# RWKV inverses in a two-layer mixer kernel: forward substitution in blocks of 8 instead of 16, and one more doubling level on TensorE

## The chip, the cores and the metric

The kernel runs on one core of a Trainium2 chip. The metric is device time in microseconds (us) of one execution, lower is better. The kernel before takes 2290.6 us, the median of three runs (2287.16 to 2292.19).

## The reference: two mixer layers, of which RWKV-7 is one of four branches

A layer normalises 256 text tokens and 1024 image tokens of 1024 channels, projects them, sends the result through four mixers (RWKV-7, S5, SSD, GLA), and projects the mixers' outputs back with a norm, a gate and a residual sum. The change lies in RWKV-7. Its reference is a scan over tokens, for two directions and four heads of 64 channels:

```
def step(S, inp):
    r_t, w_t, k_t, v_t, kk_t, a_t = inp
    sa = jnp.einsum('bhvk,bhk->bhv', S, -kk_t)
    S = S * w_t[:, :, None, :] + sa[..., None] * (kk_t * a_t)[:, :, None, :] + v_t[..., None] * k_t[:, :, None, :]
    y = jnp.einsum('bhvk,bhk->bhv', S, r_t) if need_out else None
    return S, y
...
y = ys[0] + ys[1]
mu = jnp.mean(y, axis=-1, keepdims=True)
var = jnp.mean(jnp.square(y - mu), axis=-1, keepdims=True)
y = ((y - mu) * lax.rsqrt(var + RW_GN_EPS)).reshape(b, L, W_BR) * p['rw_ln_w'] + p['rw_ln_b']
y = y + (bonus[0] + bonus[1]).reshape(b, L, W_BR)
return y * jax.nn.silu(gate), (finals[0], finals[1])
```

The kernel does not scan token by token. It takes 64 tokens at once: with A the strictly triangular 64 x 64 matrix of interactions between the tokens of such a chunk, all updates of the chunk follow from one multiplication by T = inverse(I - A).

## The kernel before: ten windows in a pipeline of five stages, laid out by a scheduler

After the in-projection and the other mixers of a layer, `rw` runs ten windows. A window is 128 tokens forward and 128 tokens backward, that is two chunks (`s`) of two directions with four heads, 16 inverses of 64 x 64 in all. Five functions make a window's stages: `rw_elem` (decays, scaled keys; DVE, ACT, POOL), `rw_pair` (the interactions A, on TensorE into the PSUM tag `pb`, masked by DVE), `rw_inv` and `rw_vals` (the inverses, the values by token), `rw_chain` (the recurrence over chunks, which multiplies by the inverse `r_TT` on PE into `pu`), `rw_out` and `rw_final`. In one iteration of the loop each stage works on another window (`ORDER`), and jobs of the S5 mixer (tiles `z_...`) go along in seven of the iterations (`SJ`).

The program text is only the input: a scheduler orders each engine's instructions by priorities and by durations that it assumes, and fixes that order when the kernel is built. So an edit of `rw_inv` can move everything that stands in the same phase.

`rw_inv` before the change: the 32 x 32 diagonal blocks of A lie in `r_Ad`, four to a column of 128 partitions. A DVE transpose writes them out with the matrix along the free axis (`r_N`), and forward substitution runs on the 16 x 16 diagonal blocks, held in `r_X`. For i = 15 down to 1 it issues two DVE instructions, a product into `r_tp` and a sum into `r_X`, each dependent on the one before:

```
for i in range(15, 0, -1):
    r0 = i // 4
    ...
    self.tt(tmp[:, :, :i, r0:], N[:, :, i, 0:i]..., X[:, :, i:i + 1, r0:4]..., OP.mult)
    self.tt(X[:, :, :i, r0:4], X[:, :, :i, r0:4], tmp[:, :, :i, r0:], OP.add)
```

Two DVE transposes make `r_DT` and `r_DN` of the result. Then two doublings follow, each of two rounds of small matmuls through the one bank of the PSUM tag `pi`. The first goes from blocks of 16 to blocks of 32: `r_Am` (the off-diagonal part of `r_Ad`, picked by POOL with a mask) times `r_DN`, an ACT copy to `r_Rm`, `r_Rm` times `r_DT`, a DVE sum into `r_DT`, a DVE transpose to `r_DN`. The second goes from 32 to 64 (`r_Bb`, `r_Rb`) into `r_TT`. A round of the first is 32 calls of 32 x 32 x 32. All of them are in f32 and show as two instructions each. Buffers: `r_Ad`, `r_N`, `r_X`, `r_Am`, `r_Rm` one each, `r_DT` and `r_DN` two, `r_A` three, PSUM tag `pi` one bank.

Of the kernel before, what the change touches and what calls it, by code (L numbers as in the profile page):

```python
# [32 lines left out]
# ---------------------------------------------------------------- column layout of w_in  # L33
# [30 lines left out]
# ---------------------------------------------------------------- per-layer parameter columns  # L64
# [21 lines left out]
# ---------------------------------------------------------------- constants that depend on shapes alone  # L86
# all along, for the projections and mixers, for RWKV
CON, ACON, RCON = {}, {}, {}
for _d, _l in ((CON, [("ident", 128), ("ones", 128), ("bones", 128), ("eps", 1), ("gneps", 1), ("one", 1)]),
               (ACON, [("triF", 128), ("triB", 128), ("gmF", 64), ("gmB", 64), ("bm4", 4), ("c16", 16), ("reset64", 256)]),  # L90
               (RCON, [("IJ", 128), ("vinit", 256), ("rm", 128), ("m16", 32), ("reset64", 256)])):
# [10 lines left out]
def constants():  # L102
# [27 lines left out]
    put("IJ", ij)  # L130
    put("m16", (np.arange(128) % 32 < 16)[:, None] & (np.arange(32) >= 16)[None])
# [92 lines left out]
# PSUM banks by tag: projections of the first layer and of the others, RWKV, out-projection  # L224
# [4 lines left out]
# tiles of a channel tile's size, of 512 columns, of S5's tables  # L229
NT_, NQ_, NH_ = (8,11,6)  # L230
# stages of the RWKV pipeline, as traced; iterations that S5 goes along with
ORDER = (3, 2, 4, 1, 0)
SJ = (3,5,6,7,9,10,11)
# order of the mixers by layer: p, q tables of S5 for this layer and the next, g GLA, s SSD, r inputs of RWKV
MO = ('pqgsr', 'gsr')
# SBUF pools from the left | from the right, by layer: what ends early lies where the next phase begins
RL = ('sm rp rl hp tp qp|re rx', 're hp tp qp rx|rp sm rl')
CL = ('oy oo ob|oa', 'oa oy oo|ob')
# engines of the residual sums and of the squares of the normed output, by pair of channel tiles
RA = "pvpv"  # L240
AA = "ppvv"
# engines of RWKV's elementwise work, by step: a ACT, p GpSimd, v DVE
EG = dict(bk="aa", ad="pppp", dg="aaaa", bb="pp", b0="p", b1="v", tk="pp", am="p", ar="vp", sp="p", bt="aa")
# tiles of the RWKV phase by size, buffers of its output
RN = (3, 2, 10)
NF = 2
# buffers of the weights, tiles projected first, by layer
WB = (4, 6)
G1 = ("misc gk", "misc gk gq")
# engines of the decays within a chunk of SSD, by direction and part  # L250
LE = "vvvv"
# order of the pools of the first layer
# [3 lines left out]
class K:  # L256
# [17 lines left out]
    def load_con(self, rwkv):  # L274
        """the constants and matrices of a phase"""
# [8 lines left out]
    def pools(self, es, nts=0, nq=0, nh=0, left=(), right=(), **psum):  # L284
        """the pools of a phase: by name, from either end of SBUF; PSUM banks by tag"""
# [23 lines left out]
    def ring(self, name, shape, n):  # L309
        """n tiles in turn, zeroed once: what is written later leaves the zeros alone"""  # L310
        ts = [self.Q(name, shape) for _ in range(n)]
        for t in ts:
            self.nc.gpsimd.memset(t, 0.0)
        return itertools.cycle(ts)
# [1499 lines left out]
```

## Time and profile before

| what | before |
|---|---|
| runs, median (lowest to highest) | 2290.6 us (2287.16 to 2292.19) |
| profiled execution, span | 2282.5 us |
| median of the runs less this span | 8.1 us |
| PE busy | 1955.0 us (86%) |
| PE weight loads busy | 1642.1 us (72%) |
| DVE busy | 1565.4 us (69%) |
| ACT busy | 933.8 us (41%) |
| POOL busy | 830.7 us (36%) |
| RWKV phase of the first layer, about | 735 to 1142 us |
| RWKV phase of the second layer, about | 1772 to 2181 us |

The profiled execution has no time of its own in the record besides its span. The span runs from its first to its last instruction; what lies around the span is in the runs' times. The two RWKV phases have 816 us between them. The engines' names: PE is TensorE, DVE VectorE, ACT ScalarE, POOL GpSimd, SP the engine that issues most DMAs.

### The profile page before, as it was taken

How to read it: one execution, taken by the hardware profiler on the slowest of the kernel's cores; microseconds unless marked ns; L12 is line 12 of the kernel's file. 1: busy time of each engine (PE TensorE's matmuls, PEld its weight loads, DVE VectorE, ACT ScalarE, POOL GpSimd, SP SyncE). 2: the span in 40 equal slices, each digit the busy share in tenths (PEclk: the TensorE clock that was granted, in tenths of full speed). 3: DMA queues.
4: the chain of work that ended last, by engine and by line, in shares of the span. 5: the costliest groups of instructions: out<-in, count | busy, mean ns of one | idle time of the engine just before them, and what ended most of it. 6: DMA issues, size and time to landing. Idle time of an engine off the chain costs nothing.

```text
span 2282.5 us, 44172 instructions
## 1 busy us (share of the span) xinstructions
PE 1955.0 (86%) x17176; PEld 1642.1 (72%) x17176; DVE 1565.4 (69%) x3513; ACT 933.8 (41%) x2016; POOL 830.7 (36%) x947
## 2 busy tenths in 40 slices
PE   7788898999975587878899999999996567888997
PEld 5577787778743466766799888887884456767797
DVE  3986867547495888897647724366665799987654
ACT  3445222223442554645423326122463456565420
POOL 1434753302246444553332203220136355454322
PEclk8689999999997688979999999999997678899898
DMA  8133544224454322422233423132412432220432
GB/s 281 44 116 122 179 152 136 65 91 140 149 164 136 112 83 80 121 64 68 94 116 94 137 90 133 55 99 86 146 50 73 145 97 85 80 75 25 139 112 93
DMA packets 208481, 246.79 MB, mean 108 GB/s; under 512 B 28816, under 2 KB 150672, under 8 KB 208272
## 3 DMA queue, kind: packets, MB, share of 16 engines
q1 hardware_dynamic: 175264, 215.52, 29.8%
q10 hardware_dynamic: 33008, 28.45, 3.8%
q8 instruction: 135, 2.21, 0.4%
q14 instruction: 74, 0.61, 0.1%
HBM read 169.29 MB, written 76.71 MB: 108 GB/s over the span
## 4 chain that ended last, share of the span: by engine, by line
PE 36%; DVE 17%; ACT 6%; issue 3%; DMA 3%; POOL 2%; SPq 0%; ACTq 0%; DVEq 0%; POOLq 0%
PE pj L321 22%; PE ps L321 3%; PE px L321 2%; PE pu L321 2%; DVE r_tp L333 2%; DVE r_X L333 2%; PE pb L321 2%; PE pc L321 1%; PE pi L321 1%; DVE r_N L1276 1%; DVE r_cs L1195 1%; PE p L321 1%; DVE z_x L333 1%; DVE r_BK L333 1%; ACT r_th L330 1%
## 5 line engine op out<-in xcount | busy, mean ns | idle before, releaser
L321 PE MATMUL pj<-hi,i_wh 128*128 128x512 f32 (+1 forms) x952 | 243.8, 377 | 18.6 <-DVE hi L1516 12.0
L321 PE MATMUL pj<-lo,i_wh 128*128 128x512 f32 (+1 forms) x952 | 240.2, 370 | 1.3 <-POOL lo L333 1.3
L321 PE MATMUL pj<-hi,i_wl 128*128 128x512 f32 (+1 forms) x952 | 239.1, 369 | 0.1
L321 PEld LDWEIGHTS pj<-hi,i_wh 128*128 128x128 f32 x952 | 169.1, 196 | 52.3 <-DVE hi L1516 12.4
L321 PEld LDWEIGHTS pj<-lo,i_wh 128*128 128x128 f32 x952 | 167.3, 193 | 32.5 <-issue 1.5
L321 PEld LDWEIGHTS pj<-hi,i_wl 128*128 128x128 f32 x952 | 167.0, 192 | 31.2 <-issue 2.6
L333 DVE TENSOR_TENSOR i_wl<-i_w,i_wh 128x512 fp32r<-128x512 f32 x108 | 82.6, 772 | 107.8 <-PE pj L321 59.9
L1539 ACT CAST i_wh<-i_w 128x512 fp32r<-128x512 f32 x108 | 66.4, 620 | 159.0 <-PE pj L321 113.4
L321 PE MATMUL pb<-r_AD,r_BK 128*128 128x256 f32 x320 | 99.9, 464 | 19.9 <-DVE r_tp L333 9.4
L321 PE MATMUL px<-r_UV,r_A 128*64 128x64 f32 x1216 | 103.9, 240 | 14.1 <-DVE r_UV L1376 10.5
L321 PEld LDWEIGHTS px<-r_UV,r_A 128*64 128x64 f32 x1216 | 88.1, 150 | 35.0 <-DVE r_UV L1376 14.6
L321 PEld LDWEIGHTS pb<-r_AD,r_BK 128*128 128x128 f32 x320 | 72.0, 237 | 37.6 <-issue 11.9
L333 DVE TENSOR_TENSOR r_X<-r_X,r_tp 128x30 f32<-128x30 f32 (+1 forms) x300 | 89.8, 299 | 6.7
L333 DVE TENSOR_TENSOR r_tp<-r_N,r_X 128x30 f32<-128x30 f32 (+1 forms) x300 | 87.6, 292 | 6.6
L321 PE MATMUL pu<-r_rs,r_TT 128*64 128x128 f32 x320 | 51.2, 311 | 35.0 <-ACT r_rs L1372 35.0
L330 ACT ACT_TABLE_LOAD x56 | 71.8, 1283 | 11.6 <-DMA z<-in_s5p 4.6
L330 ACT ACTIVATE i_o<-pj,omu 128x512 f32<-128x512 f32 (+1 forms) x46 | 28.5, 622 | 115.4 <-PE pj L321 113.8
L333 DVE TENSOR_TENSOR g_Y<-pc,g_Y 64x256 f32<-64x256 f32 x70 | 29.5, 421 | 65.0 <-ACT g_Y L536 35.3
L333 POOL TENSOR_TENSOR r_S<-r_S,r_PM 64x256 f32<-64x256 f32 x72 | 53.0, 737 | 56.6 <-DVE r_S L333 43.1
L321 PE MATMUL pj<-i_wh,hi 128*128 128x256 f32 x448 | 67.2, 288 | 6.4 <-ACT i_o L330 4.0
L336 POOL TENSOR_SCALAR r_AD<-r_AR 64x512 f32<-64x512 f32 (+1 forms) x80 | 56.7, 709 | 40.8 <-PE pb L321 31.9
L321 PEld LDWEIGHTS pu<-r_rs,r_TT 128*64 128x64 f32 x320 | 40.1, 155 | 41.4 <-ACT r_rs L1372 39.5
(458 smaller groups left out, 5172.6 us busy)
## 6 DMA issues: line engine op xcount, KB each, us to landing
i_w<-in_win SPq DMA_DIRECT2D x108, 256.0 KB, 3.0
i_o<-in_ada SPq DMA_DIRECT2D x96, 256.0 KB, 4.6
r_in<-rm SPq DMA_DIRECT2D x36, 512.0 KB, 4.2
rm<-i_o SPq DMA_DIRECT2D x48, 256.0 KB, 2.5
o_y<-yd SPq DMA_DIRECT2D x36, 256.0 KB, 3.2
z_st<-s5t SPq DMA_DIRECT2D x32, 256.0 KB, 2.7
o_w<-in_wout SPq DMA_DIRECT2D x32, 256.0 KB, 2.9
z_st<-s5t SPq DMA_DIRECT2D x24, 320.0 KB, 5.1
```

The costliest lines, as they stand in the source:

```text
L321: self.nc.tensor.matmul(out, lhsT, rhs, start=start, stop=stop, skip_group_check=True)
L330: self.nc.scalar.activation(out=out, in_=in_, func=f, **kw)
L333: (self.nc.vector if e == "v" else self.nc.gpsimd).tensor_tensor(out, a, b, op)
L336: (self.nc.vector if e == "v" else self.nc.gpsimd).tensor_scalar(out, a, s1, s2, op0, op1)
L1195: nc.vector.tensor_tensor_scan(cs[:, v], c("reset64"), t2[:, v], 0.0, OP.mult, OP.add)
L1276: nc.vector.transpose(Nt[:, :1024].rearrange("p (i j) -> p i j", j=32), AD.rearrange("p u t -> p t u").unsqueeze(2).to_broadcast([128, 32, ...
L1539: self.nc.scalar.copy(hi[:, v], w)
```

## The change: fewer substitution steps, one more doubling

Forward substitution now works on blocks of 8 (four of them per partition instead of two), so that i runs from 7 to 1: 14 DVE instructions in the place of 30 per window. The doubling from `r_Am` now runs twice, first from 8 to 16 with a new mask `m8`, then from 16 to 32 with `m16`. The transpose to `r_DN` stands at the head of each doubling and once behind them. Added per window: one POOL multiplication, one DVE transpose, one DVE sum, one ACT copy, 64 matmul calls. `r_Am` gets a second buffer; the other buffer counts stay.

```diff
-               (RCON, [("IJ", 128), ("vinit", 256), ("rm", 128), ("m16", 32), ("reset64", 256)])):
+               (RCON, [("IJ", 128), ("vinit", 256), ("rm", 128), ("m8", 32), ("m16", 32), ("reset64", 256)])):
...
-        Am = self.R("r_Am", [128, 8, 32])
-        self.tt(Am, AD, c("m16").unsqueeze(1).to_broadcast([128, 8, 32]), OP.mult, EG["am"])
-        N = Nt.rearrange("p (b f) -> p b f", b=2)[:, :, :512].rearrange("p b (i j) -> p b i j", j=32)
-        X = Xt.rearrange("p (b f) -> p b f", b=2)[:, :, :128].rearrange("p b (i r) -> p b i r", r=8)
-        tmp = self.R("r_tp", [128, 2, 16, 4], 2)
-        for i in range(15, 0, -1):
+        Am = [self.R("r_Am", [128, 8, 32], 2) for _ in range(2)]
+        for a, m in zip(Am, ("m8", "m16")):
+            self.tt(a, AD, c(m).unsqueeze(1).to_broadcast([128, 8, 32]), OP.mult, EG["am"])
+        N = Nt.rearrange("p (b f) -> p b f", b=4)[:, :, :256].rearrange("p b (i j) -> p b i j", j=32)
+        X = Xt.rearrange("p (b f) -> p b f", b=4)[:, :, :64].rearrange("p b (i r) -> p b i r", r=8)
+        tmp = self.R("r_tp", [128, 4, 8, 2], 2)
+        for i in range(7, 0, -1):
             r0 = i // 4
-            sh = [128, 2, i, 4 - r0]
-            self.tt(tmp[:, :, :i, r0:], N[:, :, i, 0:i].unsqueeze(3).to_broadcast(sh), X[:, :, i:i + 1, r0:4].to_broadcast(sh), OP.mult)
-            self.tt(X[:, :, :i, r0:4], X[:, :, :i, r0:4], tmp[:, :, :i, r0:], OP.add)
+            sh = [128, 4, i, 2 - r0]
+            self.tt(tmp[:, :, :i, r0:], N[:, :, i, 0:i].unsqueeze(3).to_broadcast(sh), X[:, :, i:i + 1, r0:2].to_broadcast(sh), OP.mult)
+            self.tt(X[:, :, :i, r0:2], X[:, :, :i, r0:2], tmp[:, :, :i, r0:], OP.add)
         DT = self.R("r_DT", [128, 32, 8], 2)
         nc.vector.transpose(DT.rearrange("p (r d) u -> p r (d u)", d=4), Xt[:, :256].rearrange("p (i r) -> p r i", r=8))
+        qs = [slice(32 * q, 32 * q + 32) for q in range(4)]
+        for a in Am:
+            DN = self.R("r_DN", [128, 8, 32], 2)
+            nc.vector.transpose(DN, DT.rearrange("p c u -> p u c"))
+            ps = self.P("pi")[:, :256].rearrange("p (u c) -> p u c", c=32)
+            for u in range(8):
+                for q in qs:
+                    self.mm(ps[q, u], a[q, u], DN[q, u])
+            Rm = self.R("r_Rm", [128, 8, 32])
+            nc.scalar.copy(Rm, ps)
+            ps = self.P("pi")[:, :256].rearrange("p (u c) -> p u c", c=32)
+            for u in range(8):
+                for q in qs:
+                    self.mm(ps[q, u], Rm[q, u], DT[q, :, u])
+            self.tt(DT, DT, ps.rearrange("p u c -> p c u"), OP.add)
         DN = self.R("r_DN", [128, 8, 32], 2)
         nc.vector.transpose(DN, DT.rearrange("p c u -> p u c"))
...
```

The scheduler's order outside the two RWKV phases and the first steps of the out-projection behind each is the same in both kernels. Two places inside show what moves.

The first place is DVE in the eighth inverse of the first layer. Before, in the middle of the substitution (`r_tp`, `r_X`), rows of other stages stand between its steps (`r_BK` is `rw_elem`, `r_UV` is `rw_chain`, `r_DT<-r_DT,pi` is the doubling of the window before):

```order
L333 TENSOR_TENSOR r_tp<-r_N,r_X 128x2x15
L333 TENSOR_TENSOR r_BK<-r_th,r_cs 128x8x64
L333 TENSOR_TENSOR r_X<-r_X,r_tp 128x2x15
L333 TENSOR_TENSOR r_tp<-r_N,r_X 128x2x14
L333 TENSOR_TENSOR r_X<-r_X,r_tp 128x2x14
L333 TENSOR_TENSOR r_tp<-r_N,r_X 128x2x13
L1376 COPY r_UV_7472<-pu 64x256
L333 TENSOR_TENSOR r_X<-r_X,r_tp 128x2x13
L333 TENSOR_TENSOR r_tp<-r_N,r_X 128x2x12
L333 TENSOR_TENSOR r_X<-r_X,r_tp 128x2x12
L333 TENSOR_TENSOR r_DT<-r_DT,pi 128x256
```

In the changed kernel the substitution of that inverse ends like this, behind its transpose to `r_N` (line numbers are one to three higher there):

```order
L334 TENSOR_TENSOR r_tp<-r_N,r_X 128x4x5
L334 TENSOR_TENSOR r_X<-r_X,r_tp 128x4x5
L334 TENSOR_TENSOR r_tp<-r_N,r_X 128x4x4
L334 TENSOR_TENSOR r_X<-r_X,r_tp 128x4x4
L334 TENSOR_TENSOR r_tp<-r_N,r_X 128x4x6
L334 TENSOR_TENSOR r_X<-r_X,r_tp 128x4x3x2
L334 TENSOR_TENSOR r_tp<-r_N,r_X 128x4x4
L334 TENSOR_TENSOR o_yl<-o_y,o_yh 128x512
L334 TENSOR_TENSOR r_X<-r_X,r_tp 128x4x2x2
L334 TENSOR_TENSOR r_tp<-r_N,r_X 128x4x2
L334 TENSOR_TENSOR r_X<-r_X,r_tp 128x4x2
L1291 STREAM_TRANSPOSE r_DT<-r_X 128x256
```

The steps now stand one behind the other with one foreign row between them, and the whole substitution is 14 rows long; the work of other stages has moved behind it.

The second place is PE in the same inverse. Before, one doubling in blocks of 16 (`r_Am`, then `r_Rm`) stands among the chain's matmuls (`pu`, `px`) and those of `rw_pair` (`pb`) and `rw_elem` (`ps`), and the step to 64 (`r_Bb`) follows:

```order
L321 MATMUL pi<-r_DN,r_Am 32x32 x32
L321 MATMUL pb<-r_AD_7212,r_BK 128x256 x4
L321 MATMUL pu<-r_rs_7694,r_TT_7422 64x128 x4
L321 MATMUL ps<-r_in,rconm 128x128 x3
L321 MATMUL pi<-r_DT,r_Rm 32x32 x14
L321 MATMUL px<-r_UV_7472,r_A 64x64 x4
L321 MATMUL pi<-r_DT,r_Rm 32x32 x18
```

In the changed kernel (`p_...` are S5's matmuls):

```order
L322 MATMUL px<-r_UV_7529,r_A 64x64 x4
L322 MATMUL pi<-r_DT,r_Rm 32x32 x32
L322 MATMUL pu<-r_UV_7529,r_Bt 128x128 x4
L322 MATMUL px<-r_UV_7529,r_A 64x64 x4
L322 MATMUL p_11466<-z_yy,rconm 128x512 x2
L322 MATMUL pi<-r_DN,r_Am 32x32 x13
L322 MATMUL px<-r_S_7769,r_AR 128x128 x4
L322 MATMUL pi<-r_DN,r_Am 32x32 x19
```

Behind the first round's second half (`r_Rm`) the second doubling's first half (`r_Am` again) stands among the chain's matmuls, with three rows of other work between the two.

## Rows read from the trace of the kernel before

**Rows 1.** The page, part 1: busy time of each engine over the span.

```profile
PE   1955.0 (86%) x17176; PEld 1642.1 (72%) x17176; DVE 1565.4 (69%) x3513; ACT 933.8 (41%) x2016; POOL 830.7 (36%) x947
```

**Rows 2.** Windows: start:end, length, busy time of PE, PEld, DVE, ACT, POOL, PEclk, DMA.

```profile
735.00:1142.00 407.00, 320.74 (x3814) 266.66 (x3813) 329.44 (x728) 216.52 (x514) 184.62 (x243) 0.84 0.29 90
...
1772.00:2181.00 409.00, 324.81 (x3861) 272.93 (x3862) 336.83 (x741) 221.97 (x526) 187.57 (x243) 0.84 0.30 93
```

**Rows 3.** Windows of 40 us in the second layer's RWKV phase, same columns.

```profile
1830.00:1870.00 40.00, 26.67 (x305) 21.58 (x304) 37.74 (x80) 23.16 (x63) 20.03 (x25) 0.71 0.36 108
...
1910.00:1950.00 40.00, 31.52 (x446) 26.68 (x446) 38.18 (x77) 16.79 (x39) 21.87 (x30) 0.74 0.25 74
...
2030.00:2070.00 40.00, 35.20 (x471) 27.50 (x469) 33.88 (x75) 28.54 (x72) 17.26 (x23) 1.00 0.22 67
...
2110.00:2150.00 40.00, 37.88 (x493) 31.78 (x492) 26.28 (x86) 16.12 (x35) 13.06 (x15) 0.83 0.21 67
```

**Rows 4.** The chain that ended last, shares by line, of 735 to 1142 us.

```profile
by line: issue 6.9%; PE px L321 6.5%; DVE r_tp L333 6.4%; DVE r_X L333 6.0%; PE pu L321 5.5%; PE pb L321 5.4%; PE ps L321 4.5%; PE pi L321 3.8%; PE p L321 3.7%; DVE r_N L1276 3.3%; ACT r_TT L1315 2.4%; DVE z_b L333 2.3%; DVE r_cs L1195 2.2%
```

**Rows 5.** The same of 1772 to 2181 us.

```profile
by line: issue 8.5%; PE pu L321 6.8%; PE px L321 6.2%; DVE r_tp L333 5.4%; DVE r_X L333 5.3%; DVE z_x L333 3.3%; PE pb L321 3.3%; DVE r_BK L333 3.1%; DVE r_N L1276 2.9%; PE ps L321 2.8%; PE pi L321 2.5%; ACT r_th L330 2.5%; DVE r_cs L1195 2
```

**Rows 6.** Groups of the substitution over the span: busy us, mean ns | idle before.

```profile
L333 DVE TENSOR_TENSOR r_X<-r_X,r_tp 128x30 f32<-128x30 f32 (+1 forms) x300 | 89.8, 299 | 6.7
L333 DVE TENSOR_TENSOR r_tp<-r_N,r_X 128x30 f32<-128x30 f32 (+1 forms) x300 | 87.6, 292 | 6.6
```

**Rows 7.** Tile `r_tp`: shortest, median and longest duration of the same instructions, ns.

```profile
L333 DVE TENSOR_TENSOR r_tp<-r_N,r_X x300: 156/198/1540, 750.6 to 2124.1; 128x24 f32<-128x24 f32 x30, 128x30 f32<-128x30 f32 x20, 128x36 f32<-128x36 f32 x20, 128x26 f32<-128x26 f32 x10
L333 DVE TENSOR_TENSOR r_X<-r_X,r_tp x300: 145/200/1544, 750.9 to 2124.3; 128x24 f32<-128x24 f32 x30, 128x30 f32<-128x30 f32 x20, 128x36 f32<-128x36 f32 x20, 128x26 f32<-128x26 f32 x10
```

**Rows 8.** Timeline of DVE, 955 to 960 us: start, duration.

```profile
956.70 0.65 DVE L333 TENSOR_TENSOR r_tp<-r_N,r_X 128x24 f32<-128x24 f32 x1
957.38 0.65 DVE L333 TENSOR_TENSOR r_X<-r_X,r_tp 128x24 f32<-128x24 f32 x1
...
959.48 0.20 DVE L333 TENSOR_TENSOR r_tp<-r_N,r_X 128x40 f32<-128x40 f32 x1
959.72 0.20 DVE L333 TENSOR_TENSOR r_X<-r_X,r_tp 128x40 f32<-128x40 f32 x1
```

**Rows 9.** Timeline of POOL in the same stretch.

```profile
956.68 1.29 POOL L336 TENSOR_SCALAR r_AD<-r_AR 64x512 f32<-64x512 f32 x2
```

**Rows 10.** Groups of the doubling from `r_Am` and of its neighbours on `pi`.

```profile
L1291 DVE STREAM_TRANSPOSE r_DN<-r_DT 128x256 f32<-128x256 f32 x20 | 12.7, 634 | 0.4
L333 DVE TENSOR_TENSOR r_DT<-r_DT,pi 128x256 f32<-128x256 f32 x20 | 8.2, 412 | 1.1 <-PE pi L321 0.9
L321 PE MATMUL pi<-r_DT,r_Rm 32*32 32x32 f32 x1280 | 25.9, 233 | 2.2 <-ACT r_Rm L1299 2.2
L321 PE MATMUL pi<-r_DN,r_Am 32*32 32x32 f32 x1280 | 17.3, 199 | 3.1 <-DVE r_DN L1291 2.7 <-DVE r_tp L333 0.2
L321 PE MATMUL pi<-r_DT,r_Rb 32*32 32x32 f32 x640 | 23.9, 234 | 1.0 <-ACT r_Rb L1321 1.0
L321 PE MATMUL pi<-r_DN,r_Bb 32*32 32x32 f32 x640 | 15.9, 202 | 8.7 <-DVE r_DN L1306 8.0 <-DVE r_X L333 0.8
L333 POOL TENSOR_TENSOR r_Am<-r_Ad,rcon 128x256 f32<-128x256 f32 x20 | 16.2, 810 | 38.6 <-PE pi L321 19.5 <-ACT r_Ad L1041 11.0 <-ACT r_rs L1372 6.3
```

**Rows 11.** Tile `r_Rm`: the copy between the two rounds, ns.

```profile
L1299 ACT COPY r_Rm<-pi x20: 354/372/401, 774.9 to 2127.1; 128x256 f32<-128x256 f32 x20
```

**Rows 12.** Timeline of one doubling, 902 to 931 us, DVE and PE.

```profile
903.03 0.64 DVE L1291 STREAM_TRANSPOSE r_DN<-r_DT 128x256 f32<-128x256 f32 x1
...
915.64 0.75 PE L321 MATMUL pi<-r_DN,r_Am 32*32 32x32 f32 x64
...
930.27 0.41 DVE L333 TENSOR_TENSOR r_DT<-r_DT,pi 128x256 f32<-128x256 f32 x1
930.72 0.65 DVE L1306 STREAM_TRANSPOSE r_DN<-r_DT 128x256 f32<-128x256 f32 x1
```

More of the change, by code (lines that the diff above doesn't have):

```diff
@@ L130, in constants @@
     put("IJ", ij)
+    put("m8", (np.arange(128) % 16 < 8)[:, None] & (np.arange(32) % 16 >= 8)[None] & ((np.arange(128) % 32 // 16)[:, None] == (np.arange(32) // 16)[None]))
     put("m16", (np.arange(128) % 32 < 16)[:, None] & (np.arange(32) >= 16)[None])
@@ L1287, in rw_inv @@
-            self.tt(X[:, :, :i, r0:4], X[:, :, :i, r0:4], tmp[:, :, :i, r0:], OP.add)
+            sh = [128, 4, i, 2 - r0]
+            self.tt(tmp[:, :, :i, r0:], N[:, :, i, 0:i].unsqueeze(3).to_broadcast(sh), X[:, :, i:i + 1, r0:2].to_broadcast(sh), OP.mult)
+            self.tt(X[:, :, :i, r0:2], X[:, :, :i, r0:2], tmp[:, :, :i, r0:], OP.add)
         DT = self.R("r_DT", [128, 32, 8], 2)
         nc.vector.transpose(DT.rearrange("p (r d) u -> p r (d u)", d=4), Xt[:, :256].rearrange("p (i r) -> p r i", r=8))
-        DN = self.R("r_DN", [128, 8, 32], 2)
@@ L1291, in rw_inv @@
-        nc.vector.transpose(DN, DT.rearrange("p c u -> p u c"))
         qs = [slice(32 * q, 32 * q + 32) for q in range(4)]
-        ps = self.P("pi")[:, :256].rearrange("p (u c) -> p u c", c=32)
-        for u in range(8):
-            for q in qs:
-                self.mm(ps[q, u], Am[q, u], DN[q, u])
-        Rm = self.R("r_Rm", [128, 8, 32])
-        nc.scalar.copy(Rm, ps)
-        ps = self.P("pi")[:, :256].rearrange("p (u c) -> p u c", c=32)
-        for u in range(8):
-            for q in qs:
-                self.mm(ps[q, u], Rm[q, u], DT[q, :, u])
@@ L1304, in rw_inv @@
-        self.tt(DT, DT, ps.rearrange("p u c -> p c u"), OP.add)
+        for a in Am:
[12 more added lines that the diff above has]
+            self.tt(DT, DT, ps.rearrange("p u c -> p c u"), OP.add)
```

## The prediction

> **What bounds the kernel now.** I read the page's busy times first. PE is busy for 86% of the span and DVE for 69% [rows 1], so over the whole program PE looks like the bound; but that is an average over stages, and the change touches two of them alone. So the next view is the windows of the two RWKV phases. There DVE has 329.4 and 336.8 us of work in 407 and 409 us (81% and 82%) and PE 320.7 and 324.8 us (79% each) [rows 2]. Neither engine is full, and they are nearly level. ACT (53% and 54%) and POOL (45% and 46%) are well below.
>
> Windows of 40 us show that the two take turns. In the early part of the second layer's phase DVE is busy for 37.7 and 38.2 us of 40 and PE for 26.7 and 31.5; in the late part PE has 35.2 and 37.9 and DVE 33.9 and 26.3 [rows 3]. The early stretches are DVE's, the late ones PE's. The granted clock goes along: 0.71 and 0.74, that is between the two levels of 1.2 and 2.4 GHz, where PE waits for DVE, and 1.00 in one of the stretches in which PE is dense.
>
> The last view is the chain that ended last. In the first phase `r_tp` and `r_X`, the two instructions of the forward substitution, have 6.4% and 6.0% of 407 us, 50.5 us together [rows 4]; in the second 5.4% and 5.3% of 409 us, 43.8 us [rows 5]. That is 94.3 us of their 177.4 us of busy time [rows 6], a share of 0.53. So a microsecond taken from the substitution is worth about half a microsecond to first order, and the substitution is the largest single item of DVE on the chain.
>
> **What is removed.** Per window 30 substitution instructions become 14, so 16 go, 320 of 600 over the 20 windows. Their sizes matter little: their median is 198 and 200 ns [rows 7] while the sizes run from 8 to 44 elements. I bound the price of one from both sides. At the mean, 16/30 of 177.4 us is 94.6 us. At the median it is 160 x 0.198 + 160 x 0.200 = 63.7 us. The difference is stretched instructions: at 956.70 us an `r_tp` of 24 elements takes 0.65 us and the `r_X` behind it 0.65 us, where their like a little later take 0.20 us [rows 8], and just then POOL runs two instructions in 1.29 us [rows 9]. If such a wait goes away with the instruction, the mean is right; if the next DVE instruction waits in its place, the median is. I take 79 us, the middle, as POOL's work does not shrink and other DVE instructions stand ready to be caught. On the chain, at 0.53, that is 42 us; the ends are 34 and 50 us.
>
> On this pair of rows the Trainium skill, SBUF — State Buffer, section "SBUF: two separate sides", has a rule: a DVE instruction with two SBUF inputs and a GpSimd instruction that reads SBUF take one shared pair of ports as an exclusive lock, and the later one waits for all of the earlier one. The trace agrees with the wait (0.65 us where 0.20 is usual, beside POOL's 1.29 us). By that rule alone the wait belongs to POOL's instruction and would be handed on to the next DVE instruction of the kind, so that the median would be the price, and the sum below would come to -7 instead of -15 us.
>
> **What is added, and what hides it.**
> - DVE: one transpose `r_DN` (634 ns) and one sum into `r_DT` (412 ns) per window, 12.7 + 8.2 = 20.9 us over 20 windows [rows 10]. They stand in the same queue as the substitution, so I give them its share of 0.53: 11 us. Ends: 0 and 20.9.
> - PE: one more round pair, 17.3 + 25.9 = 43.2 us [rows 10]. For its share on the chain I take that of the present `pi` matmuls: 3.8% of 407 and 2.5% of 409 us, 25.7 us [rows 4, 5], of 17.3 + 25.9 + 23.9 + 15.9 = 83.0 us busy [rows 10], or 0.31. That gives 13 us. Ends: 0, where PE waits for DVE anyway, and 43.2, where PE is the bound.
> - ACT: a copy `r_Rm` of 372 ns, 7.4 us [rows 11]. ACT is half idle; I take 2 us, ends 0 and 7.4.
> - POOL: a mask multiplication `r_Am`. The mean of 810 ns holds one waiting, so 16.2 us [rows 10] is an upper end. POOL stood idle for 38.6 us ahead of the present ones [rows 10] and their product is wanted only after the whole substitution, so it hides behind that; without this cover it would cost its 16.2 us. It also holds DVE up a little. I take 1 us.
> - The new buffer of `r_Am`, the wider `rcon` (32 columns more in a load once per phase) and the unchanged transpose to `r_N` I cost at nothing: no row on the chain stands for them but `r_N`, which stays.
> - The serial path of one inverse: 16 dependent instructions at a spacing of 0.24 us [rows 8] are 3.8 us less. The second doubling adds at least 0.75 us of PE [rows 12], some 0.4 of ACT, 1.3 of PE at 25.9 us / 20, 0.41 of DVE and 0.65 of transpose, 3.5 us. So the bare latency stays. The changed order puts other matmuls between the rounds, as the one before does, so the latency as it runs will be longer than that: the doubling that begins with the transpose at 903.03 us ends at 931.4 us, 28 us for 3.5 us of work [rows 12]. What would be late for it is the chain's `pu` matmul of that window, which needs `r_TT` one iteration later, and behind it on PE all that follows in order. An iteration lasts some 40 us, so I take it that most of this fits, and I add nothing.
>
> On the small matmuls the Trainium skill speaks against the change. TensorEngine Tiling (Array Packing), section "Instruction Overhead", says that a matmul has an overhead of about 60 cycles, and that one of a single column takes as long as one of 60. An estimate by this page: 128 instructions per window at 60 cycles of 2.4 GHz, 25 ns, are 3.2 us, 64 us over all windows, and at the share of 0.31 the sum would be -8 instead of -15 us. The trace does not agree: 64 of them take 0.75 us, 12 ns each [rows 12], so I give this no chance of its own.
>
> **The sum.** -42 + 11 + 13 + 2 + 1 = -15 us. Against the profiled span of 2282.5 us that is 2267.5 us. The median of the runs, 2290.6 us, is 8.1 us above the span, and I assume that this stays: 2275.6, rounded to 2276 us, 0.6% faster.
>
> **The rivals.** A measurement of this kernel can tell about 0.2%, some 4.6 us, from no change.
> - *DVE is the whole bound of the early stretches.* If six windows of each phase are DVE's, as [rows 3] suggest, each gains the full 79 / 20 - 20.9 / 20 = 2.9 us, 35 us for twelve, and at the mean price 3.7 us, 44 us. The eight late windows pay some 0.31 x 2.16 us each, 5 us. Net -30 to -39, about 2255 us. For it: 37.7 and 38.2 us of 40. Against: the substitution has only half of its time on the chain. Chance 0.17.
> - *Moderate gain, the forecast.* About -15 us, from -9 to -30. Chance 0.33.
> - *The waits are handed on.* Each stretch that a removed instruction took over its median falls on the next one, so that only 63.7 us of DVE go: -34 + 11 + 13 + 2 + 1 = -7, about 2284 us. For it: POOL's work stays, and even grows by 0.8 us per window. Against: an emptier DVE meets POOL less often. This is what the rule of SBUF — State Buffer in the Trainium skill, named above, would give. Chance 0.10.
> - *Nothing comes of it.* DVE's time is given back as idle time because the scheduler's order lets DVE wait for the two rounds on `pi`: two sums into `r_DT` per window now wait for PE, where one did for 0.9 us in all [rows 10]. The price at which the gain is gone is 0.7 us more of waiting per window. About 2290 us. Chance 0.18.
> - *PE becomes the bound: slower.* DVE's work falls to about 300 to 310 us per phase while PE's rises by 21.6 us to 342 and 346 us, 84% of the present length. If PE's 43.2 us lie wholly on the path and the removal brings the lower end: -34 + 11 + 43 + 2 + 1 = +23, about 2313 us. It decides once PE's share on the chain is over (42 - 11 - 3) / 43.2 = 0.65 instead of 0.31. For it: late stretches with PE at 37.9 of 40 us and in-order queues, in which each round's first matmul can hold up the chain's `pu` behind it. Against: PE's own clock has room in the early stretches. Chance 0.22.
>
> **How the numbers follow.** The predicted time is that of the likeliest case, 2276 us. Faster by over 0.2% (below 2286) is 0.17 + 0.33 + 0.10 = 0.60; within 0.2% 0.18; slower 0.22. Cases of both signs hold most of the chance, so the range reaches into both. The low end is 2250 us, below the first rival's 2255. The high end is 2302 us, half of the last rival. The forecast's own range is 2261 to 2282 us.
>
> **What would show it.** In the changed profile: `r_tp` and `r_X` with 280 instructions and about 75 to 100 us in place of 177; their mean near 300 ns if the waits go with them, higher if the waits are handed on. `r_DN` from the doublings and the sum into `r_DT` with 40 each, `pi` from `r_Am` and `r_Rm` with 2560 each and about 86 us together. DVE's busy time in the two phases some 55 to 65 us lower, PE's 43 us higher, the phases themselves 5 to 10 us shorter each, mostly in their early part. The prediction is wrong if PE's idle time ahead of `pi` or `pu` grows by tens of us (a wait took the place of the work), if the phases' late part grows by more than the early one shrinks, or if other DVE instructions get longer by what was saved.

## The result: 2339 us, 2.3% slower, and the profile after

The changed kernel takes 2339.2 us, the median of four runs (2336.40 to 2346.01), where the kernel before took 2291.1 us beside it (2287.16 to 2292.19). The ratio is 1.0229, with a 95% interval of 1.0200 to 1.0257. I had said 2276 us, and 2250 to 2302 us as the range.

Part 1 of the page of the changed kernel (span 2344.2 us):

```profile
PE 2004.6 (86%) x19736; PEld 1684.1 (72%) x19736; DVE 1508.5 (64%) x3233; ACT 941.1 (40%) x2036; POOL 839.6 (36%) x967
```

Its two RWKV phases, the profile's windows in the columns of [rows 2]:

```profile
742.00:1163.00 421.00, 336.43 (x5099) 280.63 (x5099) 303.88 (x595) 218.92 (x522) 188.91 (x253) 0.86 0.27 86
1790.00:2240.00 450.00, 348.19 (x5125) 293.38 (x5124) 301.50 (x594) 224.18 (x534) 186.97 (x251) 0.82 0.27 84
```

Against [rows 2] the phases are 14 and 41 us longer. The work moved as the prediction said: DVE has 605.4 instead of 666.3 us in them, PE 684.6 instead of 645.6. But PE is busy for 79% of the two phases together, as before, and DVE has fallen from 82% to 70%. The freed 61 us of DVE are idle time now, and no engine has become full. So the next view is what the engines wait for. Groups of the substitution and of the `pi` rounds over the span, as in [rows 6, 10]:

```profile
L334 DVE TENSOR_TENSOR r_X<-r_X,r_tp 128x16 f32<-128x16 f32 (+4 forms) x140 | 40.1, 286 | 3.9
L334 DVE TENSOR_TENSOR r_tp<-r_N,r_X 128x16 f32<-128x16 f32 (+4 forms) x140 | 36.1, 258 | 3.5
L322 PE MATMUL pi<-r_DT,r_Rm 32*32 32x32 f32 x2560 | 51.2, 233 | 6.2 <-ACT r_Rm L1302 4.3 <-issue 1.9
L322 PE MATMUL pi<-r_DN,r_Am 32*32 32x32 f32 x2560 | 36.3, 198 | 8.0 <-DVE r_DN L1296 8.0
L322 PE MATMUL pi<-r_DT,r_Rb 32*32 32x32 f32 x640 | 22.7, 234 | 14.5 <-ACT r_Rb L1324 14.4
L322 PE MATMUL pi<-r_DN,r_Bb 32*32 32x32 f32 x640 | 14.4, 195 | 8.1 <-DVE r_DN L1309 8.1
L1346 PE MATMUL pi<-con,r_v 128*128 128x128 f32 x40 | 10.8, 362 | 18.6 <-ACT r_TT L1330 18.5
L334 DVE TENSOR_TENSOR r_DT<-r_DT,pi 128x256 f32<-128x256 f32 x40 | 16.5, 413 | 11.5 <-PE pi L322 11.0
L334 POOL TENSOR_TENSOR r_Am<-r_Ad,rcon 128x256 f32<-128x256 f32 x40 | 34.1, 858 | 71.1 <-PE pi L322 65.1 <-ACT r_Ad L1042 5.4
```

The substitution takes 76.2 us instead of 177.4, and `r_Am` and `r_Rm` take 87.5 us of PE instead of 43.2. What is new stands behind the last bar: PE waits 36.8 us ahead of the four groups of rounds, where it waited 15.0 us in [rows 10], and besides 18.6 us ahead of the transposes of the values (`rw_vals`), which come last on `pi`, where it waited 2.7; POOL waits 65.1 us for PE before `r_Am`, where it waited 19.5. The row of the values before:

```profile
L1343 PE MATMUL pi<-con,r_v 128*128 128x128 f32 x40 | 10.1, 342 | 2.7 <-ACT r_TT L1327 2.7
```

One inverse shows what this means. The timeline of the changed kernel from 1964 us on, rows of DVE, PE and ACT. The first row, the `r_DN` at 1990.19 and the last row belong to one window; the other `pi` rows are the window before it, and `p`, `r_eP` are other stages' work.

```profile
1964.86 0.61 DVE L1291 STREAM_TRANSPOSE r_DT<-r_X 128x256 f32<-128x256 f32 x1
...
1972.19 0.55 PE L322 MATMUL pi<-r_DN,r_Am 32*32 32x32 f32 x40
...
1990.19 0.58 DVE L1296 STREAM_TRANSPOSE r_DN<-r_DT 128x256 f32<-128x256 f32 x1
1990.32 0.69 PE L322 MATMUL pi<-r_DN,r_Bb 32*32 32x32 f32 x32
...
1997.33 1.15 PE L322 MATMUL pi<-r_DT,r_Rb 32*32 32x32 f32 x32 [1.77 <-ACT r_Rb L1324]
...
2002.35 0.80 PE L322 MATMUL p<-z_x,z_st 128*128 128x128 f32 x2 [2.61 <-DVE z_x L334]
2003.73 0.63 ACT L331 ACTIVATE r_eP<-r_cs 128x512 f32<-128x512 f32 x1 [5.71 <-DVE r_cs L1196]
2005.37 0.36 ACT L1330 COPY r_TT<-pi 32x256 f32<-32x256 f32 x1
2006.31 0.80 PE L322 MATMUL p<-z_x,z_st 128*128 128x128 f32 x2 [3.16 <-DVE z_x L334]
2009.46 0.63 PE L1346 MATMUL pi<-con,r_v 128*128 128x128 f32 x2
...
2010.56 1.18 ACT L1348 COPY r_UV<-pi 64x512 f32<-64x512 f32 x2 [0.37 <-PE pi L1346]
2014.75 0.55 PE L322 MATMUL pi<-r_DN,r_Am 32*32 32x32 f32 x40
```

The substitution of the new window is done at 1965.5 us. Its first matmul on `pi` comes 49 us later. Its `r_DN` is ready at 1990.77, and its matmul then still waits 24 us: the window before holds `pi` from 1972.19 to the end of the copies to `r_UV` at 2011.74, 39.6 us. Within that stretch the rounds wait for their place in each engine's fixed order: the copy to `r_TT` stands behind ACT's `r_eP`, which waited 5.71 us for DVE; the values stand behind S5's matmuls (`p`), which waited 2.61 and 3.16 us for `z_x`. None of these waits is work of the doubling. The same part of the kernel before, one inverse:

```profile
1958.75 0.65 DVE L1289 STREAM_TRANSPOSE r_DT<-r_X 128x256 f32<-128x256 f32 x1
...
1965.93 0.75 PE L321 MATMUL pi<-r_DN,r_Am 32*32 32x32 f32 x64
...
1990.81 1.18 ACT L1345 COPY r_UV<-pi 64x512 f32<-64x512 f32 x2
1994.82 0.75 PE L321 MATMUL pi<-r_DN,r_Am 32*32 32x32 f32 x64
```

Here the first matmul on `pi` comes 6.5 us after the substitution, the bank is held for 26.1 us, and the next window takes it 28.9 us after the first. In the changed kernel the same distance is 42.6 us. The ten inverses of the second layer follow one behind another. The first window's first round starts at 1838.0 us before and 1842.8 us after (the first starts in the tile view of `pi` for the two phases):

```profile
L321 PE MATMUL pi<-r_DN,r_Am x640: 184/191/258, 1838.0 to 2126.4; 32*32 32x32 f32 x160
```

```profile
L322 PE MATMUL pi<-r_DN,r_Am x1280: 184/191/258, 1842.8 to 2194.2; 32*32 32x32 f32 x183
```

The tenth window's first round, from the timelines, before and after:

```profile
2125.86 0.75 PE L321 MATMUL pi<-r_DN,r_Am 32*32 32x32 f32 x64 [0.15 <-DVE r_DN L1291]
```

```profile
2185.95 0.55 PE L322 MATMUL pi<-r_DN,r_Am 32*32 32x32 f32 x40
```

That is 288 us before and 343 us after: 55 us more, 6.1 us for each of the nine steps from window to window. In the first layer the mean step grew less, from 37.6 to 39.9 us.

The inverse shown is worse than the mean. Taken from the starts and ends in the traces, over the first nine windows of each layer, `pi` is held for 30.6 and 27.2 us before (first and second layer) and for 36.0 and 33.5 us after, in steps of 37.6 and 32.0 us before and 39.9 and 38.1 us after. So the bank is held for most of a step in both kernels. What differs is whether finished work stands and waits for it: from the end of the transpose `r_DT<-r_X` to the window's first matmul on `pi` it is 5.5 us before and 31.2 us after, the means of the 20 windows. I call this the wait of a ready inverse.

### The profile page after: what moved, and what is told of

The parts are those of the page before. It is cut to its first block, busy times and chain, and to the rows that moved or that the text cites. A ratio compares the mean times of both kernels' runs of the same rounds, so it can differ in the third digit from the quotient of the medians.

```text
span 2344.2 us, 49065 instructions
## 1 busy us (share of the span) xinstructions
PE 2004.6 (86%) x19736; PEld 1684.1 (72%) x19736; DVE 1508.5 (64%) x3233; ACT 941.1 (40%) x2036; POOL 839.6 (36%) x967
## 5 line engine op out<-in xcount | busy, mean ns | idle before, releaser
L322 PE MATMUL pj<-hi,i_wh 128*128 128x512 f32 (+1 forms) x952 | 244.6, 378 | 18.6 <-DVE hi L1519 12.0
L322 PE MATMUL pb<-r_AD,r_BK 128*128 128x256 f32 x320 | 92.6, 437 | 4.9 <-DVE r_BK L334 2.7
L322 PEld LDWEIGHTS pb<-r_AD,r_BK 128*128 128x128 f32 x320 | 66.9, 221 | 16.6 <-POOL r_BK L334 3.0
L337 POOL TENSOR_SCALAR r_AD<-r_AR 64x512 f32<-64x512 f32 (+1 forms) x80 | 59.3, 742 | 49.6 <-PE pb L322 37.6
L322 PE MATMUL ps<-r_in,rconm 128*128 128x128 f32 x320 | 54.5, 323 | 18.5 <-ACT r_a L331 15.7
L334 POOL TENSOR_TENSOR g_pa<-g_P 64x256 f32<-64x256 f32 x36 | 31.2, 866 | 99.6 <-DVE g_P L529 70.1
L322 PEld LDWEIGHTS pj<-i_wh,hi 128*128 128x128 f32 x448 | 58.9, 192 | 10.6 <-ACT i_o L331 5.2
L322 PEld LDWEIGHTS ps<-r_in,rconm 128*128 128x128 f32 x320 | 49.7, 231 | 23.4 <-ACT r_a L331 18.7
L322 PE MATMUL pj<-i_wh,lo 128*128 128x256 f32 x448 | 64.9, 286 | 0.0
```

The source lines that it names most:

```text
L322: self.nc.tensor.matmul(out, lhsT, rhs, start=start, stop=stop, skip_group_check=True)
L334: (self.nc.vector if e == "v" else self.nc.gpsimd).tensor_tensor(out, a, b, op)
L337: (self.nc.vector if e == "v" else self.nc.gpsimd).tensor_scalar(out, a, s1, s2, op0, op1)
```

## The experiments

**Theory.** A window holds the one bank `pi` from its first round to its values, and the windows pass through it one behind another. Two more rounds lengthen the hold, by their work and by the wait of each for its place in the engines' fixed orders. **Rival:** PE's added 43 us are on the path. The ratios stand against the kernel before on the same chip, whose medians there are 2286.4 to 2286.8 us. Where two changed kernels are compared, their medians are. The change itself costs 48 us by its two medians and 52 us by its ratio of 1.0229.

**1. The removal alone** (against the changed kernel: the doubling from 8 to 16 is left out).

```diff
-        Am = [self.R("r_Am", [128, 8, 32], 2) for _ in range(2)]
-        for a, m in zip(Am, ("m8", "m16")):
+        Am = [self.R("r_Am", [128, 8, 32])]
+        for a, m in zip(Am, ("m16",)):
```

> Blocks of 8 in the substitution, but only the doubling with m16: the first doubling is left out, so the inverses lack the interactions inside blocks of 16. This is the removal alone: 16 fewer DVE instructions per window and no new round on pi. Theory of the bank (the rounds of one window, one behind the other through the single bank of pi, set the period of the windows): the number of rounds is as before, so little is gained beyond the first window's shorter substitution, 2270 to 2290 us. Theory of the forecast (DVE time on the chain): 42 us gained, 2240 to 2258 us.

2257.1 us, ratio 0.9893 (0.9851 to 0.9934): -30 us. That is at the very end of what the theory of DVE's time said, and the theory of the bank, with 2270 to 2290 us, missed. The term was priced at -42 (34 to 50).

**2. The addition alone** (blocks of 16 as before, and a first doubling with an empty mask).

```diff
+    put("m8", np.zeros((128, 32)))
...
+        for a, m in zip(Am, ("m8", "m16")):
+            self.tt(a, AD, c(m).unsqueeze(1).to_broadcast([128, 8, 32]), OP.mult, EG["am"])
...
+        for a in Am:
```

> Blocks of 16 as before, plus a doubling with an empty mask ahead of the real one, so the result is that of before. This is the addition alone. Theory of the bank: two more rounds per window on pi cost as much as in the changed kernel, and the substitution that comes back costs little, 2335 to 2365 us. Theory that PE's 43 us of work are the cost (0.31 to 1.0 of them on the chain, with 11 us of DVE): 2315 to 2345 us, and then the removal in the changed kernel would have given nothing, or, if the removal gave its 42 us, this kernel must be at 2375 to 2385 us.

2394.9 us, ratio 1.0488 (1.0458 to 1.0518): +108 us, above what either theory said, and four times the 27 us of my sum. PE's added work is 63.0 us in the page (2018.0 against 1955.0) and DVE's 17.6 us (1583.0 against 1565.4), so work alone does not fill it. The two do not add up either: -30 + 108 is +78, and the change is +48 to +52. Taken from the kernel with the addition (2394.9 to 2339.2 us), the same removal brings 56 us.

**3 and 4. Rounds and work apart.** From the addition, the extra doubling's small matmuls became four wide ones per round:

```diff
+            if a is Am[0]:
+                for q in qs:
+                    self.mm(ps[q].rearrange("p u c -> p (u c)"), a[q, 0], DN[q].rearrange("p u c -> p (u c)"))
```

> The kernel before with the second doubling added at an empty mask, as in the addition alone, but its 128 matmuls per window are 8 of 256 columns: the transpose, the two evacuations through the pi bank, the copy r_Rm and the sum into r_DT stay, while TensorE's instructions for it fall from 2560 to 160. If the addition costs so much because each round waits its turn in the in-order queues (latency of rounds), most of its cost stays: 2350 to 2395 us. If it is TensorE's work and its many small instructions, most of it goes: 2295 to 2325 us.

From the kernel before, each matmul of its one doubling was issued twice:

```diff
-        for u in range(8):
+        for u in 2 * list(range(8)):
```

> The kernel before with each matmul of the one doubling issued twice in its own round: TensorE gets 2560 instructions and about 43 us more, but no round, wait, copy or sum is added. Latency of rounds: little, 2290 to 2320 us. TensorE's work: nearly as much as the whole addition, 2350 to 2400 us.

The rounds with fewer matmuls: 2340.1 us, 1.0235 (1.0214 to 1.0256), +54. It lies between the two ranges that I had named, so neither theory alone has it. The matmuls without rounds: 2310.6 us, 1.0116 (1.0092 to 1.0141), +24, as the latency of rounds said. The first is not as clean as I meant it. Its wide calls still take PE's time: 13.4 us in the group of the second round, and some 12 us in that of the first (29.7 us with the small ones, which have 17.3 in [rows 10]).

```profile
L322 PE MATMUL pi<-r_DN,r_Am 32*32 32x32 f32 (+1 forms) x1440 | 29.7, 221 | 8.2 <-DVE r_DN L1296 4.0 <-DVE r_X L334 3.0 <-DVE r_tp L334 1.2
...
L322 PE MATMUL pi<-r_DN,r_Rm 32*32 32x256 f32 x160 | 13.4, 407 | 2.2 <-ACT r_Rm L1306 2.1
```

In the second the two groups take more PE time by this:

```profile
L321 PE MATMUL pi<-r_DT,r_Rm 32*32 32x32 f32 x2560 | 48.8, 233 | 1.7 <-ACT r_Rm L1299 1.7
L321 PE MATMUL pi<-r_DN,r_Am 32*32 32x32 f32 x2560 | 31.8, 195 | 0.6 <-issue 0.3 <-DVE r_DN L1291 0.2
```

That is 80.6 less 43.2, or 37 us. So 37 us of matmuls without rounds cost 24 us, and 26 us of matmuls with rounds 54. Half of the 108 us went with the small matmuls all the same. PE's work is part of the price, and not the whole.

**5. A hop without PE**, behind the sum into `r_DT` of the kernel before.

```diff
+        self.act(Rm, DT.rearrange("p c u -> p u c"), AF.Copy, scale=0.0)
+        self.tt(DT, DT, Rm.rearrange("p u c -> p c u"), OP.add)
```

> The kernel before with one copy on ScalarE (r_DT times 0 to r_Rm, 0.4 us) and one sum on VectorE (0.4 us) added in the dependent path behind the sum into r_DT: 16 us of work on two engines over all windows, two changes of engine, no TensorE. If any hop between engines in the inverse is dear: 2310 to 2340 us. If only rounds that go through TensorE's queue and the pi bank are: 2290 to 2305 us. If TensorE's work is what counts: no change within 0.5%, 2286 to 2298 us.

2318.5 us, 1.0137 (1.0111 to 1.0163): +32 us for two instructions a window. They took 672 and 594 ns, 25 us in all. By its interval the price is 25 to 37 us, so a microsecond in the dependent path of the inverse costs at least a microsecond, on engines that are 41% and 69% busy.

**6 to 8. The bank relieved in part.** `pi` in two halves of 256 columns by the window's parity, the values in two steps with four copies instead of two, for the changed kernel and for the one before; and the values moved to the bank `ps`.

```diff
+    def PI(self, W):
+        ...
+        return self.rz["pi"][W["w"] % 2]
```

> The changed kernel, with the one bank of pi used as two halves of 256 columns, one for even and one for odd windows; the values by token go through the same half in two steps of 256 columns (four copies of ACT in place of two). Theory of the bank: the next window's first doubling may run while this window's last rounds still hold the other half, so 20 to 60 us go, 2280 to 2320 us, unless the scheduler's order keeps the windows apart all the same. Theory of PE's work: no change, 2332 to 2347 us, or slower by the two more ACT copies per window.

> The kernel before, blocks of 16, with the pi bank used as two halves of 256 columns by the window's parity (values by token in two steps, four copies instead of two). If the one bank pi that windows share held up the kernel before as it did the changed one (23 us there): 2262 to 2285 us. If the bank is only tight once there are two doublings: 2285 to 2297 us, and two more ScalarE copies per window may cost up to 10 us.

> The changed kernel, with the transposes of the values moved from the bank of pi to the bank of ps (that of the decays and outputs). One of seven uses leaves pi. Theory of the bank: the use lasts from the last copy into r_TT to the copies into r_UV, 4 to 8 us per window with its wait, so 30 to 80 us go if nothing else takes over, 2270 to 2310 us; ps can take some of it back. Theory of PE's work, or of matmuls that wait in PE's queue for ACT: no change, 2332 to 2347 us.

Halves: 2316.6 us, 1.0146 (1.0105 to 1.0186), 23 us below the changed kernel, within the range of the theory, but not in its way. In none of the 18 steps from window to window does a first round start while the window before holds the other half; it starts 1.6 to 3.5 us behind the last copy to `r_UV`, as in this step:

```profile
1959.48 0.75 ACT L1354 COPY r_UV<-pi 64x256 f32<-64x256 f32 x2 [0.28 <-PE pi L1352]
...
1962.75 0.75 PE L328 MATMUL pi<-r_DN,r_Am 32*32 32x32 f32 x64
```

A ready inverse still waits 29.0 us. So the number fits by luck, and where the 23 us come from is not shown. The kernel before with halves: 2310.4 us, 1.0105 (1.0077 to 1.0134), 24 us slower, which the theory did not say. What the values in two steps cost by themselves was not measured. Values on `ps`: 2354.0 us, 1.0303 (1.0272 to 1.0335), a miss: 15 us above the changed kernel. That bank also serves the inputs of `rw_elem`; I did not take this apart.

**9 to 12. The same work in another order.** The inverse written ahead of the chain and the values behind it; or the values ahead of the inverse.

```diff
-ORDER = (3, 2, 4, 1, 0)
+ORDER = (2, 3, 5, 4, 1, 0)
...
-                    self.rw_vals(W)
+                elif st == 5:
+                    self.rw_vals(W)
```

> The changed kernel with the same work, but the inverse of the next window is written ahead of the chain of this one and its values behind the chain, so that its rounds come earlier in each engine's queue. If the length of the inverse from the first use of pi to the last, rounds that wait in the queues, sets the period of the windows: shorter inverses and 2295 to 2330 us. If TensorE's work sets it, no change: 2333 to 2347 us. If any other order of the same work costs 20 us or more by itself, because the order before was chosen by trial: 2350 us or more.

> The kernel before with the same new order (inverse, chain, values). Same work. If the inverse through pi sets the period before too: faster, 2255 to 2280 us. If only with two doublings: within 0.5% of 2287 us. If any other order costs something by itself: 2300 us or more.

> The changed kernel with the same work, but the values of a window are written ahead of its inverse: they take pi first, and the inverse's rounds follow, with the chain of the window before already issued. It is a second other order of the same work. By the latency of the inverse: the pi bank is then free as soon as r_TT is copied, 2310 to 2335 us. By TensorE's work: 2333 to 2347 us. If any other order costs something by itself: 2350 us or more.

> The kernel before with values written ahead of the inverse. Same work. By the latency of the inverse: 2270 to 2287 us. If only with two doublings: within 0.5% of 2287 us. If any other order costs something by itself: 2300 us or more.

The inverse ahead: 2318.5 us for the changed kernel, 1.0140 (1.0103 to 1.0177), 21 us less than without it, and 2284.4 us for the one before, 0.9994 (0.9973 to 1.0016). The values ahead: 2450.7 us, 1.0718 (1.0688 to 1.0748), and 2386.3 us, 1.0439 (1.0409 to 1.0468), both where I had put "any other order costs something by itself". That is 100 us more for the kernel before without one instruction added, nearly the price of the whole addition. Its timeline shows what is held:

```profile
2017.83 0.69 PE L1343 MATMUL pi<-con,r_v 128*128 128x128 f32 x2
...
2048.13 0.58 ACT L1345 COPY r_UV<-pi 64x512 f32<-64x512 f32 x1
...
2050.40 0.75 PE L321 MATMUL pi<-r_DN,r_Am 32*32 32x32 f32 x64
```

The values lie in `pi` for 30 us, until the chain of the window before is done with the one buffer `r_UV`; only then the inverse begins. By the latency of the inverse I had expected 2270 to 2287 us, a miss in sign: the values that come first hold the bank longer, not shorter. It also shows that an order alone can cost 100 us, so that small differences between such kernels hold the scheduler's choices too. The kernel before with halves moved by 24 us without a cause that I can name; steps of that size, taken one by one, prove little.

**13 to 16. Two whole banks for `pi`**, one for `pb`, without and with the inverse ahead; and the halves with the inverse ahead.

```diff
-PS = dict(px=2, pu=1, p5=1, pi=1, pb=2, ps=1)
+PS = dict(px=2, pu=1, p5=1, pi=2, pb=1, ps=1)
```

> The kernel before with two PSUM banks for pi and one for pb instead of one and two: nothing else. By the single bank as the bound of the changed kernel alone: the kernel before has gaps of 9 to 18 us between two uses of pi, so it gains little, and one bank pb costs something: 2280 to 2310 us.

> The changed kernel with two banks for pi and one for pb. If the single bank that every round of every window passes through is what binds: no slower than the kernel before with the same banks, and below 2300 us. If the rounds wait in the in-order queues whatever the bank: still 40 us or more above the kernel before with the same banks, 2325 to 2360 us.

> The changed kernel with two banks for pi, one for pb, and the inverse written ahead of the chain. If bank and order are two ways to the same thing (an earlier inverse): about the time of the two banks alone, within 10 us. If the queues are a second, separate cost: 15 to 30 us below it.

> The changed kernel with the halves of the pi bank and the inverse ahead of the chain, which gave 23 and 21 us each alone. If they are two ways to the same thing: 2305 to 2320 us. If they are separate costs: 2285 to 2303 us.

The kernel before with two banks: 2285.8 us, 0.9989 (0.9971 to 1.0008). The changed kernel: 2305.0 us, 1.0083 (1.0054 to 1.0111), 34 us less than with one. So it lies between what the two theories said, 19 us above the kernel before with the same banks.

Its ready inverses wait 10.7 us instead of 31.2. Yet in none of its 18 steps does a window start on `pi` ahead of the end of the copies to `r_UV` of the one before: two banks alone do not let the windows run side by side, they shorten the hold, to 31.6 and 31.7 us in the two layers, and PE no longer waits ahead of the values (0.0 us instead of 18.6).

With the inverse ahead as well: 2280.7 us, 0.9968 (0.9952 to 0.9984), another 24 us less, with a wait of 5.5 us as in the kernel before; here 5 of the 18 steps start ahead of the end of those copies. So with two banks the place in the queues looks like a second cost beside the bank's, though 24 us is also the size of the swing without a known cause. With halves and the inverse ahead: 2316.8 us, 1.0130 (1.0088 to 1.0172), no better than halves alone; there the two gave one thing, and halves don't do what two banks do.

**17 and 18. What the doubling costs then**: the kernel before, and the addition, both with two banks and the inverse ahead.

> The kernel before with two banks for pi, one for pb, and the inverse ahead of the chain. If bank and order were only tight for two doublings: within 0.4% of the kernel before, 2277 to 2296 us. If they help any kernel: 2225 to 2260 us.

> The kernel before with the second doubling added at an empty mask, two banks for pi, one for pb, and the inverse ahead of the chain. If bank and queue position made up the cost of the addition: 2300 to 2330 us, that is 20 to 45 us over the kernel before with the same banks and order, about its work. If the rounds cost what they do wherever they stand: 2370 us or more.

2283.3 us, 0.9982 (0.9966 to 0.9998), and 2320.6 us, 1.0155 (1.0127 to 1.0184). The addition costs 37 us in place of 108, and against it the removal (2280.7 less 2320.6) brings 40 us. A ready inverse waits 26.0 us in the addition with one bank and 5.9 us here. So the banks and the order do not help any kernel alike, and the rounds do not cost the same wherever they stand.

The profile of the best, the changed kernel with two banks and the inverse ahead (span 2280.8 us): its two RWKV phases, then, from the timeline, PE and ACT at the change from one window to the next.

```profile
738.00:1143.00 405.00, 333.15 (x5175) 276.95 (x5176) 308.28 (x607) 221.42 (x526) 193.05 (x257) 0.89 0.30 94
1783.00:2180.00 397.00, 329.53 (x5079) 273.49 (x5080) 293.38 (x580) 214.29 (x505) 189.37 (x247) 0.86 0.27 83
```

```profile
1909.76 1.15 PE L322 MATMUL pi<-r_DT,r_Rb 32*32 32x32 f32 x32
1910.85 0.44 PE L1347 MATMUL pi<-con,r_v 128*128 128x128 f32 x2
...
1912.92 0.36 ACT L1331 COPY r_TT<-pi 32x256 f32<-32x256 f32 x1
1913.20 0.57 ACT L1349 COPY r_UV<-pi 64x512 f32<-64x512 f32 x1
1913.34 0.75 PE L322 MATMUL pi<-r_DN,r_Am 32*32 32x32 f32 x64 [0.51 <-ACT r_TT L1331]
```

The step shown is one of the five. The next window's first round starts at 1913.34, 0.06 us after the copy to `r_TT` ends and while `r_UV` is still being copied from the other bank; in the changed kernel it came 9.0 us after the copy to `r_TT` and 3.0 us after that to `r_UV`. The values follow `r_Rb` at once, with no wait for `r_TT`. In this kernel POOL waits 16.1 us for PE before `r_Am` instead of 65.1:

```profile
L334 POOL TENSOR_TENSOR r_Am<-r_Ad,rcon 128x256 f32<-128x256 f32 x40 | 34.0, 865 | 30.1 <-PE pi L322 16.1 <-ACT r_Ad L1042 13.3
```

## Why the prediction was wrong, point by point

- **The failing step** is the last item of what is added: the serial path of one inverse, where I wrote "I take it that most of this fits, and I add nothing". It was priced against the chain's `pu` matmul, one iteration later. What was late first was not `pu` but the next window's inverse, which needs the same bank. I had the row in hand: the doubling that takes 28 us for 3.5 us of work [rows 12], in a period of some 30 to 40 us. The first 12 of these 28 us were already a wait: `r_DN` was ready at 903.67, the window before had `pi` until the end of its copies at 911.95 (the row below), and the first matmul came at 915.64. Between the holds of two windows only 7.0 and 4.8 us were free on the mean of the two layers, and the second doubling lengthened the hold by 5.4 and 6.3 us. Shown by the runs: the addition costs 108 us with one bank in the given order and 37 us with two banks and the inverse ahead, so 71 us of it go with the hold of `pi` and the place of the rounds in the queues. For the changed kernel as a whole, two banks gave 34 us, the inverse ahead 21 us, both together 58.5 us.

```profile
910.77 1.18 ACT L1345 COPY r_UV<-pi 64x512 f32<-64x512 f32 x2
```

- **The removal** was sized right in kind: -42 (34 to 50). It brought 30 us alone, 56 us beside the addition with one bank, and 40 us beside it with two banks and the inverse ahead. Its two factors were both off and made up for each other: the substitution's busy time fell by 101 us to 76.2 us, not by 79, above the 94.6 us of the mean price, and in the removal alone 103 us of it (177.4 to 74.1) went for 30 us of time, a share of 0.29, not 0.53. A ready inverse waits 13 us for `pi` there, so part of what the substitution gave was lost ahead of the bank.
- **The added work** was priced at 27 us, and its ends were 0 and 71.5 us without POOL's; 37 us is what it costs with two banks and the inverse ahead, where the ready inverse waits as little as in the kernel before. PE's part at 13 us was too small: as many matmuls without a round cost 24 us for 37 us of work, a share of 0.65 on the path instead of 0.31.
- **The change with two banks and the inverse ahead** measured 2280.7 against 2283.3 us, no difference that the two intervals show. (That -40 + 37 gives these -3 us is no test: both terms come from the same three runs.) So even there the change was worth nothing, where I had forecast -15 us by a gain that was sized too large beside a price that was sized too small, while the sign and the 48 to 52 us came from the step priced at nothing.
- **The rivals.** The slower one, PE as the bound at 2313 us, had the direction and a part of the cause: the share of 0.65 is just where I let it begin to decide. But at that share it gives 37 x 0.65 = 24 of the 108 us, PE is 79% busy in both kernels' phases, and the same PE instructions fit into 2281 us of span. The cause stood nearest to "nothing comes of it", which names waits on `pi`; I let them only eat up the gain, where the price at which it was gone was 0.7 us a window and a step from window to window grew by 2.4 us in the first layer and by 6.1 us in the second. The waits were not handed on to any extent that counts: the median of `r_tp` is 181 ns and its mean 258 ns instead of 292, so the stretched ones went along with the rest, and the DVE groups other than the substitution and the doublings' transposes and sums took 9 us more in all, where that rival would hand on 31 us (94.6 less 63.7). I had drawn this rival from the rule of the Trainium skill, SBUF — State Buffer, section "SBUF: two separate sides", on the pair of ports that a DVE and a GpSimd instruction take as an exclusive lock. That the wait passes on to the next DVE instruction was my own conclusion, and the runs do not bear it out.
- **What I had named as signs:** counts, busy times of DVE and PE came out as said (DVE 61 us less, PE 39 us more in the phases, where I had named 55 to 65 and 43). The phases did not get 5 to 10 us shorter each. The sign for being wrong came too: PE's idle time ahead of the four rounds and the values on `pi` grew from 17.7 to 55.4 us.
- **What stays open:** how the 71 us divide between bank and queues in detail, since each new order is also another choice of the scheduler; where the 23 us of the halves come from, when the windows stay apart; why the kernel before loses 24 us with halves, and why halves gain nothing more from the new order; and why the values on `ps` did worse. More buffers for `r_Am`, `r_Rm` or `r_UV` with one bank were not tried.

One rule of the Trainium skill points this way, PSUM — Partial Sum Buffer, section "Summary: rules for kernel authors": to read PSUM while a matmul runs, aim the matmul at a different bank, or at least at a different quadrant. The runs agree in part: one more bank is worth 34 us to the changed kernel and nothing that can be measured to the kernel before (0.9989).

## What to carry to other kernels

When a change moves work from one long chain of cheap instructions into rounds that cross engines, price each round at the time that a present one takes in the trace, not at the sum of its instructions, and ask which single buffer or bank is held through all of them. A long hold does not tell by itself: here the bank was held for most of a step before the change too, and a second one gave that kernel nothing. Look whether finished work stands and waits for the resource (5.5 us before, 31.2 us after). Where the room between two holds is as small as what the change adds, look before the change for a second bank and for what stands ahead of the last use of the resource in each queue.

## What the runs showed that I had not expected

The same 2560 + 2560 small matmuls, and all else that PE does, took 2004.6 us of PE in the changed kernel and 1975.6 us with two banks and the inverse ahead. The granted clock in the phases rose with it, from 0.86 and 0.82 to 0.89 and 0.86, between the levels of 1.2 and 2.4 GHz. So where PE waited less, its own work was shorter, too. And two instructions of 0.67 and 0.59 us on engines with room cost 1.6 us per window (1.3 to 1.9) when they stand in the path of the inverse.
